# Streamed pieces fetched before the resident sum, square on ScalarE, last tiles transposed one step sooner

## The chip, the cores and the metric

The kernel runs on one NeuronCore of a Trainium2 chip. TensorE multiplies matrices, VectorE, ScalarE and GpSimd work on vectors, and SyncE (SP) issues nearly all transfers between HBM and the core's SBUF. The metric is the device time of one execution in microseconds. Before the change it is 2450.3 us, the median of three runs from 2446.16 to 2452.24.

## The reference

One decoder layer on 2048 tokens of width 1024 (plus 16 meta tokens whose rows are dropped at the end): layer norm, a projection that feeds an S5 state-space mixer and a retention mixer side by side, an output projection, a layer norm, then the MLP that this change is about, and a last layer norm.

```python
h = layer_norm(h, ln_in_g, ln_in_b)
...
    mixed = jnp.concatenate([y_s5, y_ret], axis=-1) @ w_out[l]
    h = layer_norm(DEEPNORM_ALPHA * h + mixed, ln1_g[l], ln1_b[l])
    ff = jnp.square(jax.nn.relu(h @ w_up[l])) @ w_down[l]
    h = layer_norm(DEEPNORM_ALPHA * h + ff, ln2_g[l], ln2_b[l])
return h[:, N_META:]
```

w_up is 1024 x 4096, w_down 4096 x 1024, all in float32.

## The kernel before

**Blocks and phases.** The tokens go through in two blocks of 1024 (eight tiles of 128). Each block runs three phases: the projections and both mixers, the output projection with its layer norm, and the MLP (`phase3`). The order of the work on every engine is written out by the program; there is no scheduler. A counter (`tick`, `defer`) places small jobs between groups of matmuls, and `feed` brings in the weights.

**Products.** Every float32 operand is split into a high part and a rest (`hi`, `lo`), and `mm3` makes three matmuls of each pair. All of them are issued at line 357. A helper casts a weight page to its high part on ScalarE (lines 205, 219) and subtracts on VectorE (lines 207, 220). Line 216 first forms sums of weight pages where a product needs one.

**The MLP.** The 4096 hidden channels are taken in eight groups of four tiles of 128. In each group an up step makes relu(x)^2 of the group's channels for all 1024 tokens, and a down step multiplies these with w_down and adds the result to `acc` for the eight token tiles, two halves each (lines 1453 and 1456). Group 0 is classic (`up_first`): eight outputs of 24 matmuls. Groups 1 to 7 use seven products in place of eight, as Strassen's scheme does (`up_seven`): the products come in the order p = 6, 1, 5, 7, 2, 4, 3, each with two PSUM banks and four pieces k, 24 matmuls in all. Products 6, 7 and 3 read sums of the activations, which `left_sums` forms during group 0's down step and stores to HBM as sums 1 to 4 (line 1312). Sum 1 is needed by every group and is loaded back to stay, over the second half of the first four channel tiles of `h1T` (line 1485, two loads of 1 MB: the resident sum, read by p = 5). Sums 2, 3 and 4 are streamed: `ring_fill` loads pieces of 256 KB, hi and lo, into buffers `q` (line 1345), four pieces for each of p = 6, 7 and 3.

**The square.** `relu2` takes a tile x in SBUF, makes max(x, 0) * x on VectorE (line 1286), casts it on ScalarE (line 1288) and subtracts on VectorE (line 1290). Where the output sits alone in a PSUM bank (all of group 0, and p = 2 of the other groups) ScalarE copies it out first (lines 1277 and 1397). The other outputs are a sum of a bank and a tile, made by VectorE at line 1401.

**The next block.** In the last group of block 0 the down step goes through the token tiles in the order 4, 0, 1, 2, 3, 5, 6, 7 (n = 0 to 7). Beside each step one tile of the next block's h is loaded (line 1437) and after the step it is transposed by TensorE into a PSUM bank `sm` of four (line 339), cast to `hi` by ScalarE (line 340) and subtracted to `lo` by VectorE (line 341). The same steps carry the last layer norm of the finished tiles: VectorE (lines 268, 301), GpSimd (lines 281, 302), ScalarE (line 289) and the store of the output (line 1470). The last tile of the block ends with `norm_end` (lines 310 and 314). Then the next block begins: it loads its `rope` tables, and its first matmuls, the gates of head 0, read the transposed tiles 0 to 3 and then 4 to 7.

**Queues.** SP issues in program order, and each issue waits for what it needs, so a load stands behind every store or load ahead of it. Eight counters (DMAHW0 to 7) are used in turn, so the ninth load after another waits until that one has landed.

Of the kernel before, what the change touches and what calls it, by code (L numbers as in the profile page):

```python
# [12 lines left out]
AF = mybir.ActivationFunctionType  # L13
ALU = mybir.AluOpType
# [15 lines left out]
NT = TB // 128  # L30
# [20 lines left out]
class Builder:  # L51
# [1210 lines left out]
    def up_first(self, b, g):  # L1262

        nc = self.nc
        h1, l1 = self.h1T
        ff = {}
        order = [(f, nb) for f in range(G) for nb in range(2)]
        if g == 0:
            order = [(f, nb) for nb in range(2) for f in range(G)]
        for f, nb in order:  # L1270
            up = self.get(("u", b, g * G + f))
            ps = self.big()
            tk = slice(nb * 512, nb * 512 + 512)
            w = lambda k, i: up[k // 4][:, i, (k % 4) * 128:(k % 4) * 128 + 128]
            self.mm3(ps, [(w(k, 0), w(k, 1), h1[:, k, tk], l1[:, k, tk]) for k in range(8)], marks=(3, 7))
            x = self.q()
            nc.scalar.copy(x, ps)
            ff.setdefault(f, {})[nb] = self.relu2(x)
            if nb == 1:
                self.free(("u", b, g * G + f))  # L1280
        return lambda f, t: [z[:, t % 4 * 128:t % 4 * 128 + 128] for z in ff[f][t // 4]]

    def relu2(self, x):

        nc = self.nc
        nc.vector.scalar_tensor_tensor(out=x, in0=x, scalar=0.0, in1=x, op0=ALU.max, op1=ALU.mult)  # L1286
        hi = self.q(F32R)
        nc.scalar.copy(hi, x)  # L1288
        lo = self.q(F32R)
        nc.vector.tensor_tensor(out=lo, in0=x, in1=hi.bitcast(F32), op=ALU.subtract)  # L1290
        self.qfree()
        return hi, lo
# [55 lines left out]
    def up_seven(self, b, g):  # L1348

        nc = self.nc  # L1350
        V, S = nc.vector, nc.scalar
        h1, l1 = self.h1T
        t1, t2 = slice(0, 512), slice(512, 1024)
        left = {1: (0, t1), 2: (4, t1), 4: (4, t2), 5: (0, t2)}
        NQ = G // 2
        ff = {f: {} for f in range(G)}
        acc, s12, s21, s22 = {}, {}, {}, {}
        for p in PORDER:
            bank = {1: "A", 2: "A", 6: "B", 7: "B", 4: "B", 5: "C", 3: "C"}[p]
            first = p in (1, 6, 5)  # L1360
            for q in range(NQ):
                if first:
                    acc[bank, q] = self.bank()
            w = [self.get(("U", b, g, q, p)) for q in range(NQ)]
            self.hold = p in (4, 3)
            for k in range(4):
                if p in left:
                    k0, tk = left[p]
                    ah, al = h1[:, k0 + k, tk], l1[:, k0 + k, tk]
                else:  # L1370
                    ah, al = self.ring.popleft()
                for q in range(NQ):
                    c = slice(k * 128, k * 128 + 128)
                    self.mm3(acc[bank, q], [(w[q][:, 0, c], w[q][:, 1, c], ah, al)],
                             first=first and k == 0, last=k == 3, more=not first)
                if p not in left:
                    self.qfree(2)
                if self.stream:
                    self.ring_fill((4 if self.bg else 6) if self.stream[0][0] != 2 else 3 if p == 3 else 0)
                if k == 1:  # L1380
                    self.tick()
            for q in range(NQ):
                self.free(("U", b, g, q, p))
                ps, fa, fb = acc[bank, q], 2 * q, 2 * q + 1
                if p == 6:
                    s12[q] = self.q()
                    S.copy(s12[q], ps)
                elif p == 1:
                    s21[q] = self.q()
                    V.tensor_tensor(out=s12[q], in0=s12[q], in1=ps, op=ADD)  # L1390
                    S.copy(s21[q], ps)
                elif p == 5:
                    s22[q] = self.q()
                    V.tensor_tensor(out=s22[q], in0=s21[q], in1=ps, op=ADD)
                elif p == 2:
                    x = self.q()
                    S.copy(x, ps)
                    ff[fa][0] = self.relu2(x)
                else:
                    x, f, h = {7: (s22, fb, 1), 4: (s21, fa, 1), 3: (s12, fb, 0)}[p]  # L1400
                    V.tensor_tensor(out=x[q], in0=x[q], in1=ps, op=ADD)
                    ff[f][h] = self.relu2(x.pop(q))
            self.tick()
        return lambda f, t: [z[:, t % 4 * 128:t % 4 * 128 + 128] for z in ff[f][t // 4]]

    def phase3(self, b):
        nc, a = self.nc, self.a
        ng = NF // G
        nc0 = CLASSIC
        more = b + 1 < NB  # L1410
# [4 lines left out]
        for g in range(ng):  # L1415
# [5 lines left out]
            last = g == ng - 1  # L1421
            ff = self.up_first(b, g) if g < nc0 else self.up_seven(b, g)
# [9 lines left out]
            xs = deque()  # L1432

            def load_h(t):
                xs.append([self.q(), self.q()])
                for hf in range(2):
                    nc.sync.dma_start(out=xs[-1][hf], in_=self.h_d[(b + 1) * NT + t][:, hf * 512:hf * 512 + 512])
            if last and more:
                load_h(to[0])
            for n, t in enumerate(to):  # L1440
                if g >= nc0 and not last and more and n == 4 and rest:
                    self.bg.append(self.rest_norm([rest.popleft() for _ in range(2)]))
                self.hold = g >= nc0 and n == 0
                if last and more and n + 1 < NT:
                    load_h(to[n + 1])
                end = last and n == NT - 1
                for hf in range(2):
                    ps = self.big() if last else self.bank()
# [8 lines left out]
                    if end:  # L1457
# [2 lines left out]
                        self.half_stats(st, self.acc[t], hf)  # L1460
                        if hf == 0:
                            self.norm_halves(self.acc[to[n - 1]], gb2)
                    if n == 3 and hf == 1 and not last:
                        self.qfree(8)
                if last:
                    if more:
                        self.to_channels(xs.popleft(), *self.hT, t * 128)
                        self.qfree(2)
                    out = a["out"][b * TB + t * 128:b * TB + (t + 1) * 128, :]
                    store = lambda t=t, out=out: nc.sync.dma_start(out=out, in_=self.acc[t])  # L1470
                    if not end:
# [7 lines left out]
                elif g >= nc0:  # L1479
                    self.ring_fill(3 if n < 3 else 4 if self.bg or more and rest else 6)  # L1480
                elif g == nc0 - 1 and n >= 4 and sums and (not self.bg or n == NT - 1):
                    sums = False
                    self.drain_bg()
                    for i in range(2):
                        nc.sync.dma_start(out=self.h1T[i].bitcast(F32)[:, 0:4, 512:1024],
                                          in_=self.s_d[b][1][:, :, i, :])
                    self.ring_fill(4)
            self.qfree(16 if last else 8)
            for f in range(G):
                self.free(("d", b, g * G + f))  # L1490
            if last:
# [72 lines left out]
```

## Time and profile before

| | value |
|---|---|
| median of three runs | 2450.3 us |
| the profiled execution | 2449.24 us, of which the span is 2447.5 us |
| mean granted clock of TensorE | 0.987 of full |
| TensorE matmul, weight load | 2344.7 us (96%), 2007.5 us (82%) |
| VectorE, ScalarE, GpSimd | 1615.6 us (66%), 668.4 us (27%), 263.4 us (11%) |

The span goes from the first to the last instruction of the profiled execution, and all times in the rows below count from its start. A timeline row gives the start, the time until the merged instructions end, the engine, the line, what is written and read, the count, and in brackets how long the engine was idle before and what ended that. Matmuls overlap, so the starts of successive groups tell more than their ends. A row of waits gives the total, the count and the longest.

### The profile page before, as it was taken

How to read it: one execution, taken by the hardware profiler on the slowest of the kernel's cores; microseconds unless marked ns; L12 is line 12 of the kernel's file. 1: busy time of each engine (PE TensorE's matmuls, PEld its weight loads, DVE VectorE, ACT ScalarE, POOL GpSimd, SP SyncE). 2: the span in 40 equal slices, each digit the busy share in tenths (PEclk: the TensorE clock that was granted, in tenths of full speed). 3: DMA queues.
4: the chain of work that ended last, by engine and by line, in shares of the span. 5: the costliest groups of instructions: out<-in, count | busy, mean ns of one | idle time of the engine just before them, and what ended most of it. 6: DMA issues, size and time to landing. Idle time of an engine off the chain costs nothing. (4 is left out here: it accounts for less than half of the span.)

```text
span 2447.5 us, 31696 instructions
## 1 busy us (share of the span) xinstructions
PE 2344.7 (96%) x11596; PEld 2007.5 (82%) x11596; DVE 1615.6 (66%) x3491; ACT 668.4 (27%) x1431; POOL 263.4 (11%) x334
## 2 busy tenths in 40 slices
PE   6889999899999999999999999999999999999998
PEld 5778889778878888888888999987887888888886
DVE  6867757666867776766585455565686666566657
ACT  3323323222321232123232222222232122212222
POOL 2322222301000000000030011100100000000004
PEclk8999999999999999999999999999999999999999
DMA  5132253352464546453442322234246343434332
GB/s 202 66 103 83 87 116 114 91 169 73 138 241 146 167 161 202 141 165 112 146 164 92 89 75 79 78 101 153 74 139 239 114 155 112 137 113 155 112 129 86
DMA packets 166972, 313.13 MB, mean 128 GB/s; under 512 B 18544, under 2 KB 59280, under 8 KB 166560
## 3 DMA queue, kind: packets, MB, share of 16 engines
q1 hardware_dynamic: 166816, 311.11, 39.4%
q8 instruction: 91, 1.49, 0.3%
q14 instruction: 65, 0.53, 0.1%
HBM read 256.25 MB, written 55.84 MB: 128 GB/s over the span
## 5 line engine op out<-in xcount | busy, mean ns | idle before, releaser
L357 PE MATMUL big<-pg,act 128*128 128x384 f32 x2304 | 457.0, 348 | 0.8 <-ACT act L340 0.6
L357 PE MATMUL big<-act,pg 128*128 128x512 f32 x1632 | 425.1, 395 | 2.4 <-DVE act L341 2.4
L357 PE MATMUL big<-pg,q 128*128 128x512 f32 x1728 | 412.2, 390 | 0.0
L357 PEld LDWEIGHTS big<-pg,act 128*128 128x128 f32 x2304 | 403.4, 192 | 4.7 <-DVE act L341 1.5
L357 PEld LDWEIGHTS big<-pg,q 128*128 128x128 f32 x1728 | 323.8, 188 | 67.1
L357 PEld LDWEIGHTS big<-act,pg 128*128 128x128 f32 x1632 | 303.9, 189 | 66.9 <-DVE act L341 2.9
L357 PE MATMUL sm<-pg,q 128*128 128x512 f32 x1344 | 322.8, 389 | 0.0
L357 PEld LDWEIGHTS sm<-pg,q 128*128 128x128 f32 x1344 | 252.3, 188 | 52.4
L281 POOL TENSOR_TENSOR ln_rs<-ln_rs,mhalf 128x1 f32<-128x1 f32 (+1 forms) x49 | 51.3, 1047 | 1481.5 <-DVE ln_rs L280 1481.4
L357 PE MATMUL sm<-act,pg 128*128 128x512 f32 x672 | 188.7, 389 | 0.0
L357 PE MATMUL big<-pg,yt 128*128 128x512 f32 x768 | 183.2, 397 | 1.6 <-DVE yt L1140 1.5
L207 DVE TENSOR_TENSOR pg<-wraw,pg 128x512 fp32r<-128x512 f32 x238 | 151.6, 688 | 39.7 <-ACT pg L205 39.7
L357 PEld LDWEIGHTS big<-pg,yt 128*128 128x128 f32 x768 | 145.1, 191 | 33.6 <-DVE yt L1140 3.3
L205 ACT CAST pg<-wraw 128x512 fp32r<-128x512 f32 x272 | 153.2, 619 | 68.1 <-DMA wraw<-in_w_down_dram 27.2
L219 ACT CAST pg<-q 128x512 fp32r<-128x512 f32 x112 | 69.4, 622 | 355.8 <-DVE q L216 355.8
L1288 ACT CAST q<-q 128x512 fp32r<-128x512 f32 x128 | 79.5, 621 | 272.3 <-DVE q L1286 257.4
L357 PE MATMUL sm<-q,pg 128*128 128x512 f32 x504 | 144.6, 395 | 7.5 <-DMA q<-sum 4.0
L1456 DVE TENSOR_TENSOR acc<-acc,big 128x512 f32<-128x512 f32 x128 | 87.0, 684 | 94.7 <-PE big L357 94.6
L1290 DVE TENSOR_TENSOR q<-q 128x512 fp32r<-128x512 f32 x128 | 88.7, 693 | 91.9 <-ACT q L1288 89.0
L357 PEld LDWEIGHTS sm<-act,pg 128*128 128x128 f32 x672 | 126.1, 188 | 26.1
L357 PE MATMUL big<-q,pg 128*128 128x512 f32 x504 | 143.8, 394 | 0.0
L220 DVE TENSOR_TENSOR pg<-q,pg 128x512 fp32r<-128x512 f32 x112 | 76.3, 692 | 82.2 <-ACT pg L219 77.8
(235 smaller groups left out, 2915.2 us busy)
## 6 DMA issues: line engine op xcount, KB each, us to landing
q<-sum SPq DMA_DIRECT2D x336, 256.0 KB, 5.3
wraw<-in_wup_dram SPq DMA_DIRECT2D x64, 512.0 KB, 4.0
wraw<-in_w_down_dram SPq DMA_DIRECT2D x64, 512.0 KB, 4.2
wraw<-in_wslab_dram SPq DMA_DIRECT2D x48, 512.0 KB, 3.6
sum<-q SPq DMA_DIRECT2D x64, 256.0 KB, 2.3
smat<-mat SPq DMA_DIRECT2D x32, 256.0 KB, 3.8
wraw<-in_w_out_dram SPq DMA_DIRECT2D x16, 512.0 KB, 3.7
acc<-h SPq DMA_DIRECT2D x16, 512.0 KB, 3.8
```

The source lines that it names most:

```text
L205: nc.scalar.copy(pg[z][:, 0, :], raw[0][:, z * 512:z * 512 + 512])
L207: e.tensor_tensor(out=pg[z][:, 1, :], in0=raw[0][:, z * 512:z * 512 + 512], in1=pg[z].bitcast(F32)[:, 0, :], op=ALU.subtract)
L219: nc.scalar.copy(pg[:, 0, :], x)
L220: self.post.append(lambda: nc.vector.tensor_tensor(out=pg[:, 1, :], in0=x, in1=pg.bitcast(F32)[:, 0, :], op=ALU.subtract))
L281: nc.gpsimd.tensor_tensor(out=rs[:n, 0:1], in0=rs[:n, 0:1], in1=self.mhalf[:n, 0:1], op=ALU.pow)
L357: nc.tensor.matmul(ps, l, r, start=(i == 0), stop=(i == n - 1), skip_group_check=more)
L1288: nc.scalar.copy(hi, x)
L1290: nc.vector.tensor_tensor(out=lo, in0=x, in1=hi.bitcast(F32), op=ALU.subtract)
L1456: nc.vector.tensor_tensor(out=acc, in0=acc, in1=ps, op=ALU.add)
```

## The change

Four things change. Line numbers of the changed kernel are a few higher (`relu2` at 1288 to 1293, `ring_fill` at 1348, the resident sum at 1493).

1. For outputs that sit alone in a bank, `relu2` takes the bank: ScalarE makes Relu out of it and then Square in place; the VectorE product is left out.
2. The first four pieces of sum 2 are fetched before the resident sum.
3. In the last group of block 0 the tiles of the next block are loaded with counts 1, 1, 1, 1, 1, 2, 0, 0 beside the steps n (and one ahead of them). The tile of n = 5 is transposed between that step's halves, the next after it, the last after n = 6.
4. Buffers of the last group are counted free after n = 4 in place of at the end.

```diff
--- before.py
+++ after.py
@@ -1273,17 +1273,20 @@
             tk = slice(nb * 512, nb * 512 + 512)
             w = lambda k, i: up[k // 4][:, i, (k % 4) * 128:(k % 4) * 128 + 128]
             self.mm3(ps, [(w(k, 0), w(k, 1), h1[:, k, tk], l1[:, k, tk]) for k in range(8)], marks=(3, 7))
-            x = self.q()
-            nc.scalar.copy(x, ps)
-            ff.setdefault(f, {})[nb] = self.relu2(x)
+            ff.setdefault(f, {})[nb] = self.relu2(ps=ps)
             if nb == 1:
                 self.free(("u", b, g * G + f))
         return lambda f, t: [z[:, t % 4 * 128:t % 4 * 128 + 128] for z in ff[f][t // 4]]
 
-    def relu2(self, x):
+    def relu2(self, x=None, ps=None):
 
         nc = self.nc
-        nc.vector.scalar_tensor_tensor(out=x, in0=x, scalar=0.0, in1=x, op0=ALU.max, op1=ALU.mult)
+        if ps is None:
+            nc.vector.scalar_tensor_tensor(out=x, in0=x, scalar=0.0, in1=x, op0=ALU.max, op1=ALU.mult)
+        else:
+            x = self.q()
+            nc.scalar.activation(out=x, in_=ps, func=AF.Relu)
+            nc.scalar.activation(out=x, in_=x, func=AF.Square)
         hi = self.q(F32R)
         nc.scalar.copy(hi, x)
         lo = self.q(F32R)
@@ -1393,9 +1396,7 @@
                     s22[q] = self.q()
                     V.tensor_tensor(out=s22[q], in0=s21[q], in1=ps, op=ADD)
                 elif p == 2:
-                    x = self.q()
-                    S.copy(x, ps)
-                    ff[fa][0] = self.relu2(x)
+                    ff[fa][0] = self.relu2(ps=ps)
                 else:
                     x, f, h = {7: (s22, fb, 1), 4: (s21, fa, 1), 3: (s12, fb, 0)}[p]
                     V.tensor_tensor(out=x[q], in0=x[q], in1=ps, op=ADD)
@@ -1435,14 +1436,19 @@
                 xs.append([self.q(), self.q()])
                 for hf in range(2):
                     nc.sync.dma_start(out=xs[-1][hf], in_=self.h_d[(b + 1) * NT + t][:, hf * 512:hf * 512 + 512])
+            def turn():
+                self.to_channels(xs.popleft(), *self.hT, nt.popleft() * 128)
+                self.qfree(2)
+            nt, nl = deque(to), deque(to)
             if last and more:
-                load_h(to[0])
+                load_h(nl.popleft())
             for n, t in enumerate(to):
                 if g >= nc0 and not last and more and n == 4 and rest:
                     self.bg.append(self.rest_norm([rest.popleft() for _ in range(2)]))
                 self.hold = g >= nc0 and n == 0
-                if last and more and n + 1 < NT:
-                    load_h(to[n + 1])
+                if last and more:
+                    for _ in range((1, 1, 1, 1, 1, 2, 0, 0)[n]):
+                        load_h(nl.popleft())
                 end = last and n == NT - 1
                 for hf in range(2):
                     ps = self.big() if last else self.bank()
@@ -1460,12 +1466,13 @@
                         self.half_stats(st, self.acc[t], hf)
                         if hf == 0:
                             self.norm_halves(self.acc[to[n - 1]], gb2)
-                    if n == 3 and hf == 1 and not last:
+                    if n == 3 + last and hf == 1:
                         self.qfree(8)
+                    if last and more and n == 5 and hf == 0:
+                        turn()
                 if last:
-                    if more:
-                        self.to_channels(xs.popleft(), *self.hT, t * 128)
-                        self.qfree(2)
+                    if more and n < NT - 1:
+                        turn()
                     out = a["out"][b * TB + t * 128:b * TB + (t + 1) * 128, :]
                     store = lambda t=t, out=out: nc.sync.dma_start(out=out, in_=self.acc[t])
                     if not end:
@@ -1481,11 +1488,11 @@
                 elif g == nc0 - 1 and n >= 4 and sums and (not self.bg or n == NT - 1):
                     sums = False
                     self.drain_bg()
+                    self.ring_fill(4)
                     for i in range(2):
                         nc.sync.dma_start(out=self.h1T[i].bitcast(F32)[:, 0:4, 512:1024],
                                           in_=self.s_d[b][1][:, :, i, :])
-                    self.ring_fill(4)
-            self.qfree(16 if last else 8)
+            self.qfree(8)
             for f in range(G):
                 self.free(("d", b, g * G + f))
             if last:
```

On SP, at the end of group 0's down step of block 0, before the change (the last stores of the sums; `act` is `h1T`, and a counter named in brackets is waited for):

```order
L1312 DMA sum0_2_127<-q_7050 128x512 [waits DMAHW0_49,Activation_49]
L1312 DMA sum0_2_127<-q_7052 128x512 [waits DMAHW1_49,DVE_49]
L1312 DMA sum0_4_129<-q_7056 128x512 [waits DMAHW2_49,Activation_49]
L1312 DMA sum0_4_129<-q_7058 128x512 [waits DMAHW3_49,DVE_49]
L1485 DMA act_5798<-sum0_1_126 128x4x512 [waits DMAHW4_49,PE_49]
L1485 DMA act_5799<-sum0_1_126 128x4x512 [waits DMAHW5_49]
L1345 DMA q_7093<-sum0_2_127 128x512 [waits DMAHW6_49]
L1345 DMA q_7094<-sum0_2_127 128x512 [waits DMAHW7_49]
```

The same place with the change:

```order
L1315 DMA sum0_4_129<-q_7058 128x512 [waits DMAHW3_49,DVE_49]
L1348 DMA q_7091<-sum0_2_127 128x512 [waits DMAHW4_49,PE_49]
L1348 DMA q_7092<-sum0_2_127 128x512 [waits DMAHW5_49]
L1348 DMA q_7095<-sum0_2_127 128x512 [waits DMAHW6_49]
L1348 DMA q_7096<-sum0_2_127 128x512 [waits DMAHW7_49,PE_49]
L1348 DMA q_7099<-sum0_2_127 128x512 [waits DMAHW0_49]
L1348 DMA q_7100<-sum0_2_127 128x512 [waits DMAHW1_49,PE_49]
L1348 DMA q_7103<-sum0_2_127 128x512 [waits DMAHW2_49]
L1348 DMA q_7104<-sum0_2_127 128x512 [waits DMAHW3_49]
L1493 DMA act_5798<-sum0_1_126 128x4x512 [waits DMAHW4_49]
L1493 DMA act_5799<-sum0_1_126 128x4x512 [waits DMAHW5_49]
```

The two loads of the resident sum moved behind the eight loads of sum 2, and they now wait for the counters of the first two of these (DMAHW4 and 5). Block 1 has the same order.

On TensorE, in the last group of block 0 (`sm<-ident,q` are transposes of the next block's tiles, `big<-pg,q` the down step, `big<-act,pg` the next block's gates), the difference:

```order
 L357 MATMUL big<-pg,q 128x512 x24
 L339 MATMUL sm<-ident,q 128x128 x8
-L357 MATMUL big<-pg,q 128x512 x24
+L357 MATMUL big<-pg,q 128x512 x12
+L339 MATMUL sm<-ident,q 128x128 x8
+L357 MATMUL big<-pg,q 128x512 x12
 L339 MATMUL sm<-ident,q 128x128 x8
 L357 MATMUL big<-pg,q 128x512 x24
 L339 MATMUL sm<-ident,q 128x128 x8
 L357 MATMUL big<-pg,q 128x512 x24
-L339 MATMUL sm<-ident,q 128x128 x8
 L357 MATMUL big<-act,pg 128x512 x48
```

The last eight transposes no longer stand right before the gates; eight stand inside step n = 5 instead.

On VectorE, the end of block 0 before the change (the adds of steps n = 6 and 7, and the split halves of the transposed tiles at line 341):

```order
L1456 TENSOR_TENSOR acc<-acc,big 128x512 x2
L341 TENSOR_TENSOR act<-sm,act 128x4x128 x2
L268 BN_STATS ln_st<-acc 128x6 x2
L279 BN_AGGR ln_mv<-ln_st 128x2
L280 TENSOR_SCALAR ln_rs<-ln_mv 128x1
L301 TENSOR_TENSOR acc<-acc,q 128x512 x2
L1456 TENSOR_TENSOR acc<-acc,big 128x512
L268 BN_STATS ln_st<-acc 128x6
L301 TENSOR_TENSOR acc<-acc,q 128x512 x2
L1456 TENSOR_TENSOR acc<-acc,big 128x512
L268 BN_STATS ln_st<-acc 128x6
L341 TENSOR_TENSOR act<-sm,act 128x4x128 x2
```

And with the change:

```order
L1462 TENSOR_TENSOR acc<-acc,big 128x512 x2
L341 TENSOR_TENSOR act<-sm,act 128x4x128 x2
L268 BN_STATS ln_st<-acc 128x6 x2
L279 BN_AGGR ln_mv<-ln_st 128x2
L280 TENSOR_SCALAR ln_rs<-ln_mv 128x1
L301 TENSOR_TENSOR acc<-acc,q 128x512 x2
L1462 TENSOR_TENSOR acc<-acc,big 128x512
L268 BN_STATS ln_st<-acc 128x6
L301 TENSOR_TENSOR acc<-acc,q 128x512 x2
L1462 TENSOR_TENSOR acc<-acc,big 128x512
L268 BN_STATS ln_st<-acc 128x6
```

The split of the last tile, at the end before, is now the pair behind the adds of step n = 6; the pair that stood there moved one step up.

## Rows read from the trace of the kernel before

**Rows 1.** The page: busy time, share of the span and instructions of each engine

```profile
PE 2344.7 (96%) x11596; PEld 2007.5 (82%) x11596; DVE 1615.6 (66%) x3491; ACT 668.4 (27%) x1431; POOL 263.4 (11%) x334
```

**Rows 2.** Waits of TensorE over the span: total us, times, longest us

```profile
PE sm L357 <- DMA q<-sum: 4.0, 2, 3.8
PE sm L357 <- DVE q L216: 3.5, 1, 3.5
PE big L357 <- DVE act L341: 2.4, 1, 2.4
```

**Rows 3.** Timeline, TensorE, end of group 0 in block 0

```profile
687.63 2.88 PE L357 MATMUL sm<-pg,q 128*128 128x512 f32 x12
690.35 2.88 PE L357 MATMUL big<-pg,q 128*128 128x512 f32 x12
696.99 1.25 PE L357 MATMUL sm<-q,pg 128*128 128x512 f32 x3 [3.75 <-DMA q<-sum]
...
704.47 0.84 PE L357 MATMUL sm<-act,pg 128*128 128x512 f32 x3
```

**Rows 4.** Windows: us, engines' busy us, PEclk, DMA share, GB/s

```profile
698.00:700.00 2.00, 2.00 (x8) 1.54 (x7) 0.00 (x0) 0.00 (x0) 0.00 (x0) 0.57 1.05 396
```

**Rows 5.** Timeline, SP and TensorE, end of group 0 in block 1

```profile
1853.01 1.25 SPq L1485 DMA_DIRECT2D act<-sum  x2
...
1856.34 2.88 PE L357 MATMUL big<-pg,q 128*128 128x512 f32 x12
...
1862.69 0.76 PE L357 MATMUL sm<-q,pg 128*128 128x512 f32 x1 [3.46 <-DVE q L216]
...
1871.56 0.84 PE L357 MATMUL sm<-act,pg 128*128 128x512 f32 x3
```

**Rows 6.** Lines 1345 and 1485 around 690 us, issue ns, landing; 1345 overall

```profile
L1345 SPq DMA_DIRECT2D q<-sum x6: 425/624/737, 688.5 to 691.7; - x6
...
DMA to landing us min/median/max: 8.1/8.3/8.5
...
L1485 SPq DMA_DIRECT2D act<-sum x2: 539/589/639, 687.2 to 687.8; - x2
...
DMA to landing us min/median/max: 6.1/7.2/8.3
...
q<-sum SPq DMA_DIRECT2D x336, 256.0 KB, 5.3
```

**Rows 7.** Timeline and loads, end of block 0 and start of block 1

```profile
1260.74 5.74 PE L357 MATMUL big<-pg,q 128*128 128x512 f32 x24
1265.99 1.29 DVE L341 TENSOR_TENSOR act<-sm,act 128x512 fp32r<-128x512 f32 x2 [0.75 <-ACT act L340]
1267.11 5.74 PE L357 MATMUL big<-pg,q 128*128 128x512 f32 x24
1276.22 1.28 DVE L1456 TENSOR_TENSOR acc<-acc,big 128x512 f32<-128x512 f32 x2
1279.84 5.96 PE L357 MATMUL big<-act,pg 128*128 128x512 f32 x25
1287.50 1.27 DVE L341 TENSOR_TENSOR act<-sm,act 128x512 fp32r<-128x512 f32 x2
1295.19 6.43 PE L357 MATMUL big<-pg,act 128*128 128x384 f32 x36
...
L1437 SPq DMA_DIRECT2D q<-h x2: 383/640/896, 1261.1 to 1261.5; - x2
...
DMA to landing us min/median/max: 4.6/4.7/4.8
...
L552 SPq DMA_DIRECT2D rope<-in_rope_dram x1: 399/399/399, 1292.2 to 1292.2; - x1
```

**Rows 8.** Groups by line: names, shapes, count, busy us, mean ns, idle before

```profile
L1286 DVE SCALAR_TENSOR_TENSOR q<-q 128x512 f32<-128x512 f32 x128 | 88.2, 689 | 2.9
L1288 ACT CAST q<-q 128x512 fp32r<-128x512 f32 x128 | 79.5, 621 | 272.3 <-DVE q L1286 257.4 <-DMA q<-sum 12.8 <-DMA q<-h 2.1
```

## The prediction

> **What bounds the kernel now.** The page's first line says it: TensorE has a matmul under way for 96% of the span, VectorE 66%, ScalarE 27% [rows 1]. So nothing that is saved on VectorE or ScalarE counts by itself; only TensorE's gaps do, and what follows each gap. The second view is the list of what TensorE waited for. In the stages that the diff touches it holds three gaps of over 2 us [rows 2]: one for a piece of a sum from HBM (3.8 us), one put down to VectorE line 216 (3.5 us), one for the split halves of the next block's transposed tiles (2.4 us).
>
> The third view, the timeline, places the gaps. The first [rows 3]: down groups start every 2.72 us (687.63, 690.35), so the next work, p = 6, was due at 693.07. It began at 696.99, waiting for q<-sum. Then the granted clock fell: 0.57 in the stretch shown [rows 4], which is TensorE at the 1.2 GHz level for most of it. The 24 matmuls of p = 6 need 2 x 2.72 = 5.44 us at the 2.4 GHz level; the first matmul of p = 1 came at 704.47. Loss: 704.47 - 693.07 - 5.44 = 5.96 us.
>
> The second gap is the same place in block 1 [rows 5]: due at 1856.34 + 2.72 = 1859.06, p = 1 at 1871.56, so 1871.56 - 1859.06 - 5.44 = 7.06 us. The table blames VectorE here (3.46 us), but line 216 makes a weight page for later p, and SP's start at 1853.01 lies as far ahead of the gap as in block 0. I read it as the same DMA wait.
>
> Why the piece is late [rows 3, 6]: SP issued the two loads of the resident sum (1 MB each) at 687.2 and 687.8, the first piece at 688.5. They landed 6.1 and 8.3 us after issue; the six loads behind them took 8.1 to 8.5, so the first was there near 696.8. Over the run such a load takes 5.3 us in the median.
>
> The third gap [rows 7]: the next block's gates start at 1279.84 and need 4 x 2.72 = 10.88 us, so the following matmuls were due at 1290.72. They came at 1295.19: 4.47 us lost. TensorE waited 2.4 us for line 341, which VectorE ran at 1287.50, since it is half a step and more behind: it added step n = 6 at 1276.22, whose matmuls began at 1267.11 and took 5.74 us, to 1272.85.
>
> The gaps that can go hold 5.96 + 7.06 + 4.47 = 17.49 us.
>
> **The change part by part.**
>
> *Pieces before the resident sum.* Nothing is added; eight loads pass two. I take SP's start from the profile, 687.2. The issues there took up to 0.74 us each [rows 6], so the second load of the first pair starts by 688.0 and the eighth by 692.4. A load of this size behind one store landed 4.6 us after issue [rows 7], the median is 5.3: the first pair is there at 692.6 to 693.3, the last by 697.7. They are due at 693.07 and 693.07 + 3 x 1.36 = 697.15. Between no wait and one of 0.2 + 0.5 us I take none, since the issues are slowest when the queue holds the 2 MB. In block 1 SP starts at 1853.01 for work due at 1859.06, so there is as much room.
>
> What is late next is the resident sum, which p = 5 reads after p = 6 and p = 1, at 693.07 + 10.88 = 703.95. In the order of the change its loads wait for the counters of the first pair and stand behind eight issues, so they go out at 693.3 and 693.9 at the latest. With the longest landing measured, 8.3, they are in by 702.2: 1.7 us to spare, in block 1 about the same. The pieces of sums 3 and 4 go out after them as before. So both losses go: 13.0 us; at the dear end 0.7 us is given back twice.
>
> *Square on ScalarE.* 16 outputs in the classic group and 28 in the p = 2 steps, 44 of 128. Each drops a VectorE operation of 689 ns (44 x 0.689 = 30.3 us) and adds a ScalarE pass; the cast of the same tile there takes 621 ns, so 44 x 0.62 = 27 us on an engine that is idle 73% of the span [rows 1, 8]. The copy out of the bank becomes a Relu out of the bank. The trace of before has no Square; the bounds are that it is free, or that it takes a cast's time twice, 54 us of ScalarE. On TensorE I cost either at nothing: the list of its waits has none for these tiles, and the p = 2 outputs are needed two more p (10.9 us) and a down step later. If the longer ScalarE row made a weight cast late the cost would be one pass, 0.6 us. The gain is bounded by 8 x 0.69 = 5.5 us of earlier sums per block, since VectorE is behind while it makes them; it widens the margins above, so I add nothing.
>
> *Tiles transposed sooner.* The number of transposes stays; two are done inside and after n = 5, one after n = 6, none after n = 7. For the last tile, line 341 now stands behind the adds of step 6: these began at 1276.22, and 1.4 us for the two halves moved ahead of them, 1.3 for the adds and 1.3 of its own make 1280.2. The second gate needs it at 1279.84 + 5.44 = 1285.28. Even three such pairs later it is in time. The loss of 4.47 us goes.
>
> What is late next there: (a) the tile for the second transposing of n = 5. SP issues it at 1261.1 and 1261.5, behind the store, and it took 4.6 to 4.8 us there: 1265.9 to 1266.3; needed at 1260.74 + 5.44 + 0.92 = 1267.1 (0.92 is what a step's transposes cost: 6.37 between step starts less 5.44). Margin 0.8. (b) The bank for it, free when line 341 has run on the tile of n = 4: 1265.99 to 1267.28. That is level with the need: 0 to 0.5 us. (c) rope, which SP loads behind the last store, at 1292.2: with the same 4.7 it lands near 1296.9. The first tile of head 0 now ends 4.47 us sooner, at 1290.72 + 6.43 x 24/36 = 1295.0, and TensorE wants it rotated after half a tile more, 1297.1, with the rotation between: 0 to 1 us. I take 0.5 us for (b) and (c) together, of 0 to 1.5.
>
> *Sum.* 17.5 - 0.5 = 17.0 us of the profiled execution's 2449.24 (span 2447.5 and some 1.7 around it): 2432.2. That execution is 1.1 us under the median of 2450.3, so the median goes to 2433.3. The uncertain part is the clock: of the losses 3.75, 3.46 and 2.4 us are idle time, so 2.2, 3.6 and 2.1 us are the slower matmuls behind them. A repeat may draw three times the least or the most of these, 6.3 to 10.8 in place of 7.9, which moves the gain to 15.4 to 19.9.
>
> The Trainium skill (TensorE: Matmul & The Clock Gate, Part 1) says that the monitor behind this clock is not aligned with the program, so that the number of slow matmuls after a gap differs from run to run. The trace bears this out as far as it goes: the 3.46 us gap cost more clock than the 3.75 us one. By that rule a median of other executions could hold less of the 7.9 us than this profile does; with none of it, the sum would be 17.0 - 7.9 = 9.1 us.
>
> **Rivals.**
> 1. *Only the two sum gaps go* (or the transposes give back their part): the mid-step transposes meet a tile or bank that is later than (a) and (b), and a gap as long as the third one comes there, with its clock. For it: margins of 0 to 0.8 us, and VectorE a step behind. Against it: line 341 for the last tile comes some 8 us earlier than before (1280.2 for 1288.8). Gain 17.0 - 4.5 = 12.5: 2437.8.
> 2. *Pieces and resident sum share the rate after all.* 4 MB must arrive within 17 us, and each p needs 512 KB per 1.36 us. If each block keeps a gap of 2.4 us with 2.2 to 3.6 of clock, 2 x 5.3 = 10.6 comes back: 6.4 us gain, 2443.9. For it: the loads took 8.3 us when the queue was full. Against: the first pieces now meet no 2 MB.
> 3. *The change doesn't do what it says:* the late piece waits for its stores, not for the 2 MB ahead of it. Then both gaps stay and 4.0 us remain: 2446.3. Against it: the landing times above, equal for act and piece.
> 4. *Slower:* the resident sum, now behind the pieces, comes after p = 5 wants it, and p = 5 is stopped in both blocks. The price is (w + 2.7) twice, w the lateness; it decides at 2 x (w + 2.7) > 17.0 + 7.4, so w above 9.5 us: landing 20 us after issue in place of 6.1 to 8.3. With w = 10: 2 x 12.7 - 17.0 = 8.4 us slower, 2458.7. For it: only that nothing in the profile shows these loads behind eight others.
>
> **How the numbers follow.** Forecast 0.70, rival 1 0.15, rival 2 0.06, rival 3 0.06, rival 4 0.03. A difference within 0.3% (7.4 us) can't be told from none here. Faster by more: forecast and rival 1, with a little of rival 2: 0.87. Same: 0.10. Slower: 0.03. The forecast's own range is 2430.4 to 2434.9 by the clock's share, 2427 to 2438 with about 3 us either way for the spread of the runs (2446.16 to 2452.24). Up to rival 2 it is 2427 to 2443.5.
>
> **What would show it.** In the profile after: no gap of TensorE before p = 6 in either block, clock 1.00 in those stretches; act<-sum issued after the eight pieces and landed before p = 5; no wait for line 341 at the gates; 44 Relu and 44 Square passes near 0.6 us on ScalarE and VectorE some 30 us less busy. It is wrong if a wait for act<-sum, for q<-h or for a bank stands in TensorE's list with more than 2 us, or if the clock falls elsewhere.

## The result, and the profile after

The changed kernel takes 2437.34 us (median of 4 runs, 2434.59 to 2439.23), the kernel before, run beside it, 2451.1 us (2446.16 to 2452.24). The ratio is 0.9947 with a 95% interval of 0.993 to 0.9964: 13.8 us less, and between 8.8 and 17.2. The forecast was a gain of 17.0, at the upper edge of that interval.

The profiled execution of the changed kernel took 2439.23 us, span 2437.4. Its busy times, beside [rows 1]:

```profile
PE 2344.9 (96%) x11596; PEld 2012.3 (83%) x11596; DVE 1590.8 (65%) x3447; ACT 697.1 (29%) x1475; POOL 263.1 (11%) x334
```

TensorE's work is the same; 24.8 us went from VectorE, 28.7 came to ScalarE. The line of the square alone lost 30.1 us (88.2 in [rows 8], 58.1 here), as forecast; why VectorE's total fell by less is not traced. The two passes, by line (names, count, busy us, mean ns of one), and the square that stayed on VectorE:

```profile
L1285 DVE SCALAR_TENSOR_TENSOR q<-q 128x512 f32<-128x512 f32 x84 | 58.1, 692 | 2.9
L1289 ACT ACTIVATE q<-q 128x512 f32<-128x512 f32 x44 | 27.8, 633 | 1.4
L1288 ACT ACTIVATE q<-big 128x512 f32<-128x512 f32 x30 | 17.8, 593 | 16.4 <-PE big L357 13.4 <-DVE acc L328 3.0
L1288 ACT ACTIVATE q<-sm 128x512 f32<-128x512 f32 x14 | 8.2, 589 | 0.0
```

Gap 1, beside [rows 3]. Timeline of TensorE, end of group 0 in block 0 (start us, duration us):

```profile
696.61 2.88 PE L357 MATMUL big<-pg,q 128*128 128x512 f32 x12
699.33 0.84 PE L357 MATMUL sm<-q,pg 128*128 128x512 f32 x3
...
704.77 0.84 PE L357 MATMUL sm<-act,pg 128*128 128x512 f32 x3
```

p = 6 begins 2.72 us after the last down group, and p = 1 follows 5.44 us later: no wait and no slow matmul. The granted clock of the window of p = 6 is 1.00 where [rows 4] had 0.57, at the same transfer rate (us; each engine's busy us; PEclk, DMA share, GB/s):

```profile
700.00:702.00 2.00, 2.00 (x10) 1.67 (x9) 1.86 (x4) 0.62 (x1) 0.00 (x0) 1.00 1.05 396
```

SP's queue there, and how long the pieces took from issue to landing (issue ns, first and last issue):

```profile
689.49 4.14 SPq L1348 DMA_DIRECT2D q<-sum  x8
693.68 1.65 SPq L1493 DMA_DIRECT2D act<-sum  x2
...
L1348 SPq DMA_DIRECT2D q<-sum x8: 376/430/719, 689.5 to 692.9; - x8
...
DMA to landing us min/median/max: 4.1/5.3/6.0
```

The first piece leaves 699.33 - 689.49 = 9.84 us ahead of its use (before: SP began with the resident sum 5.83 us ahead) and lands in 6.0 at most, in place of over 8 [rows 6]. In block 1 the lead is 9.84 us again, and p = 6 runs through, beside [rows 5]:

```profile
1846.25 4.71 SPq L1348 DMA_DIRECT2D q<-sum  x8
...
1856.09 0.84 PE L357 MATMUL sm<-q,pg 128*128 128x512 f32 x3
...
1861.53 0.84 PE L357 MATMUL sm<-act,pg 128*128 128x512 f32 x3
```

Gap 3, beside [rows 7]: the gates of block 1 run through, 1280.01 to 1290.88, and the wait for line 341 is gone. But a new wait stands 8 us behind. TensorE, then VectorE and SP:

```profile
1280.01 11.04 PE L357 MATMUL big<-act,pg 128*128 128x512 f32 x48
1290.88 6.43 PE L357 MATMUL big<-pg,act 128*128 128x384 f32 x36
1299.00 0.30 PE L663 MATMUL sm<-ident,qk 128*128 128x128 f32 x1 [1.69 <-DVE qk L654]
...
1297.57 0.42 DVE L651 TENSOR_TENSOR t<-big,rope 128x256 f32<-128x256 f32 x1 [1.41 <-DMA rope<-in_rope_dram]
...
1292.06 0.99 SPq L316 DMA_DIRECT2D out_dram<-acc  x2
1293.15 0.41 SPq L552 DMA_DIRECT2D rope<-in_rope_dram  x1
```

The rope table still leaves SP behind the last stores, and now VectorE waits for it. Ahead of the gates TensorE also waits 1.73 us for the fifth tile (q<-h). That wait is not new: it took 1.21 us in the kernel before and 1.67 in its second profile.

**How the executions were compared.** The spans of the two profiles differ by only 10.1 us, since this one came to the first up projection of block 0 at 610.48 us, the kernel before at 604.22, and the change leaves all the code up to there alone. So only stretches between two marks are compared, and what a kernel without that wait needs is taken as zero. These are: from the first up projection of block 0 (the mark) to p = 1, 94.29 us; the gates, 10.87; from there to the second rotated transposes, 11.13; from the first transposes of acc in block 1 to p = 1 there, 151.39. What each execution needed beyond that, in us, idle time and slow matmuls together:

```
kernel                       mark   gap 1  gates  rope  gap 2  mark to end
before                       604.22  5.96   4.48  0.00   7.04   1843.3
before again                 607.30  3.75   4.19  0.00   5.98   1840.5
order alone                  608.82  0.00   2.62  0.02   0.00   1829.7
square alone                 606.36  0.48   4.25  0.03   1.11   1831.6
tiles alone                  606.07  6.45   0.01  2.10   5.71   1837.9
tiles alone, again           608.37  5.24   0.01  2.30   5.99   1839.2
changed                      610.48  0.00   0.00  1.86   0.00   1826.9
changed again                605.69  0.00   0.01  3.96   0.00   1828.6
changed without order        605.63  0.50   0.01  0.03   1.14   1828.8
changed without tiles        608.48  0.00   2.30  0.00   0.00   1829.5
changed, rope on ScalarE     606.33  0.00   0.01  1.18   0.00   1826.5
the same again               608.13  0.01   0.01  1.12   0.00   1823.7
rope, and feed held          605.05  0.01   0.01  0.03   0.00   1830.6
rope, and tile load ahead    607.95  0.00   0.01  1.26   0.00   1826.0
```

### The profile page after: what moved, and what is told of

Its sections match the earlier page's. It is cut to its first block, busy times and chain, and to the rows that moved or that the text cites. A ratio compares the mean times of both kernels' runs of the same rounds, so it can differ in the third digit from the quotient of the medians.

```text
span 2437.4 us, 31642 instructions
## 1 busy us (share of the span) xinstructions
PE 2344.9 (96%) x11596; PEld 2012.3 (83%) x11596; DVE 1590.8 (65%) x3447; ACT 697.1 (29%) x1475; POOL 263.1 (11%) x334
## 5 line engine op out<-in xcount | busy, mean ns | idle before, releaser
L357 PE MATMUL big<-pg,act 128*128 128x384 f32 x2304 | 463.6, 351 | 0.8 <-ACT act L340 0.6
L357 PEld LDWEIGHTS big<-pg,act 128*128 128x128 f32 x2304 | 410.2, 195 | 4.6 <-issue 1.4
```

Source lines behind the costliest of these rows:

```text
L357: nc.tensor.matmul(ps, l, r, start=(i == 0), stop=(i == n - 1), skip_group_check=more)
```

## The experiments

Theory A is the prediction's sum: the order of the loads closes gaps 1 and 2, the tiles gap 3, the square adds nothing. Theory B came from the trace after: the square brings the sums some 4 us forward, and that by itself would close most of gaps 1 and 2. Part 4 of the change (buffers counted free sooner) goes with the tiles in every run below; the prediction gave it no price, and no run shows it alone.

**1. Order alone.** In the kernel before:

```diff
                     self.drain_bg()
+                    self.ring_fill(4)
                     for i in range(2):
                         nc.sync.dma_start(out=self.h1T[i]..., in_=self.s_d[b][1][:, :, i, :])
-                    self.ring_fill(4)
```

> Only the order: the pieces of the streamed sum are fetched ahead of the resident sum, square and tile schedule as before. Theory A (the order is what closes the two waits before p = 6): both waits go, 5.96 us in block 0 and 7.06 us in block 1, so about 13.0 us less than before (2438); the SyncE queue issues the first piece 5.8 to 6.1 us ahead of p = 6, as before's first load was. Theory B (the earlier sums do most of it): a piece issued 5.8 us ahead that lands 5.3 to 8.5 us after its issue is still up to 2.5 us late, so PE waits up to 2.5 us in each block and the gain is 8 to 13 us (2438 to 2443). The wait of the gates on the ScalarE chain (4.47 us in before) stays under both.

2439.15 us against 2448.15, ratio 0.9957 (0.9944 to 0.9969): 9.0 us less. Both gaps are gone. SP, the landing of the pieces, and TensorE:

```profile
691.13 3.83 SPq L1345 DMA_DIRECT2D q<-sum  x8
...
DMA to landing us min/median/max: 3.7/5.4/6.0
...
697.67 0.84 PE L357 MATMUL sm<-q,pg 128*128 128x512 f32 x3
```

6.54 us of lead and 6.0 of landing at most. In block 1 the lead was 5.94, the landing 5.5. So A is right on the order and B's doubt falls: it suffices without the square, but only just. By size, 9.0 us is short of A's 13.0; the interval reaches from 7.6 to 13.7.

In block 1 p = 6 now begins before VectorE has run line 216 at all, which [rows 2] blamed for that gap:

```profile
1857.03 0.84 PE L357 MATMUL sm<-q,pg 128*128 128x512 f32 x3
...
1857.84 0.69 DVE L216 TENSOR_TENSOR q<-wraw 128x512 f32<-128x512 f32 x1
```

**2. Square alone.** In the kernel before, the outputs out of a bank:

```diff
-            x = self.q()
-            nc.scalar.copy(x, ps)
-            ff.setdefault(f, {})[nb] = self.relu2(x)
+            ff.setdefault(f, {})[nb] = self.relu2(ps=ps)
...
+            nc.scalar.activation(out=x, in_=ps, func=AF.Relu)
+            nc.scalar.activation(out=x, in_=x, func=AF.Square)
...
```

(and the same for p = 2).

> Only Relu and Square on ScalarE in place of the square on VectorE; order of the loads and tile schedule as before. Theory A: nothing (2449 to 2451), both waits before p = 6 stay 2 us or longer because the resident sum still stands ahead of the pieces. Theory B: the last sums are stored about 4 us sooner, so the first load leaves SyncE 9.8 us ahead of p = 6 instead of 5.8 to 6.1; the first piece, 1.3 to 1.7 us behind it, lands 8.1 to 8.5 us later, hence 0 to 0.5 us late: most of both waits goes by this part alone, 12 to 13 us less than before (2437 to 2439).

2439.78 us against 2448.15, ratio 0.996 (0.9947 to 0.9974): 8.4 us less. Theory A's "adds nothing" is wrong for the part by itself, and B's 12 to 13 is more than the median shows. In block 1, with the resident sum still ahead:

```profile
1845.69 1.29 SPq L1486 DMA_DIRECT2D act<-sum  x2
1847.04 14.86 SPq L1348 DMA_DIRECT2D q<-sum  x17
...
DMA to landing us min/median/max: 8.4/8.9/9.0
...
1856.12 1.32 PE L357 MATMUL sm<-q,pg 128*128 128x512 f32 x3 [0.43 <-DMA q<-sum]
```

The pieces are as slow as before, 9.0 us at most, but leave 8.65 us ahead of their use at 1855.69: 0.43 us late.

**3. The changed kernel without the order:**

```diff
                     self.drain_bg()
-                    self.ring_fill(4)
...
+                    self.ring_fill(4)
```

> The changed kernel with the order undone: resident sum ahead of the pieces again, square on ScalarE and tile schedule kept. Theory A: both waits before p = 6 come back, about 13 us over the changed kernel (2450). Theory B: the first piece leaves 8.2 us ahead of p = 6 and lands 0 to 0.5 us late, so 0 to 1.5 us over the changed kernel (2437 to 2439).

2437.02 us against 2448.15, ratio 0.9951 (0.9938 to 0.9963), the changed kernel's ratio within the error: A's 2450 is wrong, B's 2437 to 2439 holds. Gaps 1 and 2 hold 0.50 and 1.14 us. So in this kernel either of the two parts nearly replaces the other: their gains overlap, they don't add. Its rope cost nothing, because the gates began 2 us late: the table left SP 0.26 us after the gates' end (1288.72 and 1288.46), in the changed kernel 2.27 us after it (1293.15 and 1290.88). The gates were late because the matmuls behind the wait for the fifth tile were slow, 12 in 4.54 us in place of 3.01:

```profile
1255.73 1.44 PE L339 MATMUL sm<-ident,q 128*128 128x128 f32 x8 [2.05 <-DMA q<-h]
1256.83 4.54 PE L357 MATMUL big<-pg,q 128*128 128x512 f32 x12
```

**4. Tiles alone**, in the kernel before (loads and transposes of the next block's tiles as in the change):

```diff
-                if last and more and n + 1 < NT:
-                    load_h(to[n + 1])
+                if last and more:
+                    for _ in range((1, 1, 1, 1, 1, 2, 0, 0)[n]):
+                        load_h(nl.popleft())
...
+                    if last and more and n == 5 and hf == 0:
+                        turn()
...
```

> Only the next block's tiles are loaded and transposed a step sooner; order and square as before. The 4.47 us wait of the gates at the end of block 0 goes under every theory. Theory A (prediction): the rope tables cost up to 1.5 us of it, taken at 0.5, so about 4.0 us less than before (2446 to 2447). Theory B (after's trace): the rope tables still leave behind the last stores, and PE waits 1.7 us for them, so 3.0 to 3.2 us less (2447 to 2448). The two waits before p = 6 stay at their length in before. If the transposes gave their part back elsewhere, 0 (2450 to 2451).

2448.96 us against 2448.15, ratio 1.0003 (0.9994 to 1.0012). That was a miss for both theories, so it was run again.

> Only the tile schedule, once more (its first timing gave 0, where its trace had lost the wait of the gates and the kernel without this part lay 3.4 us over the changed one). Theory B (the part is worth 3 us by itself, and the first timing was a low draw of before or a high one of it): 2 to 4 us less than before run beside it. Theory C (it gives its gain back when VectorE still squares): 0 again, and then this profile shows the return between the gates of block 1 and the end.

2447.51 us against 2449.02, ratio 0.9993 (0.9984 to 1.0002). In both traces the wait of the gates is gone and TensorE waits for the rotation instead; the second one's:

```profile
1283.73 11.04 PE L357 MATMUL big<-act,pg 128*128 128x512 f32 x48
...
1303.17 0.30 PE L663 MATMUL sm<-ident,qk 128*128 128x128 f32 x1 [2.13 <-DVE qk L654]
```

By the table the part gains 2.3 to 4.5 us at the gates and gives 1.9 to 4.0 back at the rope (nothing in one execution), where 0 to 1.5 was foreseen. What is left, about 1.5 us (means in the next section), is too little for these runs to tell from none. That something else takes the rest is neither shown nor excluded.

**5. The changed kernel without the tiles,**

```diff
-                if last and more:
-                    for _ in range((1, 1, 1, 1, 1, 2, 0, 0)[n]):
-                        load_h(nl.popleft())
+                if last and more and n + 1 < NT:
+                    load_h(to[n + 1])
...
```

beside **the changed kernel again**, unedited:

> The changed kernel without the earlier loads and transposes of the next block's tiles (order and square kept). Theory A (prediction's terms): the gates wait 4.5 us again and the rope's 0.5 is saved, 4.0 us over the changed kernel. Theory B (after's trace: the rope wait takes 1.3 of it): 2.7 to 3.2 us over. Theory C (as the run with that part alone was timed): 0. By the trace all three show the wait of the gates on L341, 2.2 to 2.4 us in the profile.

> The changed kernel once more, for its spread and a second profile. No edit. If the 6.3 us by which the changed kernel's first up projection of block 0 began later than in before (610.5 against 604.2 us, in code that the change leaves alone) is a matter of the execution, this profile shows it anywhere between 604 and 611 us, and the rest of the span (from there to the end) is 1827 us again, within 1.5. If it belongs to the changed kernel, it is 610 again.

2438.08 us without the tiles (ratio 0.9958, 0.9944 to 0.9972), 2434.68 with them (0.9945, 0.9932 to 0.9957): 3.4 us apart, with overlapping intervals. So these runs do not decide between the 4.0, the 2.7 to 3.2 and the 0 of the three theories. The changed kernel's second run repeats its gain, 14.5 us of 2449.16. Its mark lay at 605.69 this time, so 610.48 belonged to the execution. The stretch from the mark to the end was 1828.6, 1.7 longer than in the first profile: here the wait for the rotation was followed by slow matmuls, 12 in 3.85 us, and the rope cost 3.96 in all.

```profile
1294.53 0.30 PE L663 MATMUL sm<-ident,qk 128*128 128x128 f32 x1 [2.21 <-DVE qk L654]
1294.69 3.85 PE L357 MATMUL big<-pg,act 128*128 128x384 f32 x12
```

Without the tiles the gates waited for line 341 again, but more cheaply than before:

```profile
1278.02 5.96 PE L357 MATMUL big<-act,pg 128*128 128x512 f32 x25
1285.83 5.53 PE L357 MATMUL big<-act,pg 128*128 128x512 f32 x23 [1.86 <-DVE act L341]
1291.19 6.43 PE L357 MATMUL big<-pg,act 128*128 128x384 f32 x36
```

**6. The kernel before again**, unedited:

> The kernel before, once more, for a second profile; no edit. The first up projection of block 0 begins anywhere between 604 and 611 us if that spread belongs to the execution, and at 604 if it belongs to the kernel; from there to the end 1843 us within 2. Both waits before p = 6 and the 4.5 us at the gates are there again.

2448.56 us against 2449.02, ratio 0.9998 (0.9989 to 1.0006). The mark is at 607.30, and from there to the end it took 1840.5 us, a little under the range foreseen. The same three gaps are there, at other prices: gap 1 took 3.75 us in place of 5.96. Its timeline:

```profile
693.44 2.88 PE L357 MATMUL big<-pg,q 128*128 128x512 f32 x12
699.38 1.29 PE L357 MATMUL sm<-q,pg 128*128 128x512 f32 x3 [3.06 <-DMA q<-sum]
700.51 0.85 PE L357 MATMUL big<-q,pg 128*128 128x512 f32 x3
```

After 3.06 us of idling three matmuls were slow; in [rows 3] it took twelve and more to come back (p = 6 lasted 7.48 us in place of 5.44).

**7. The rope table on the ScalarE queue**, in the changed kernel, for block 1:

```diff
-        nc.sync.dma_start(out=self.rope, in_=a["rope"][b])
+        e = nc.scalar if b else nc.sync
+        e.dma_start(out=self.rope, in_=a["rope"][b])
         self.mask = p1.tile([128, 128], F32, name="mask")
-        nc.sync.dma_start(out=self.mask, in_=a["mask"])
+        e.dma_start(out=self.mask, in_=a["mask"])
```

> The changed kernel with block 1's rope table and mask loaded from the ScalarE queue (issued after the last tile's scaling, at about 1285.5 us) and no longer from SyncE behind the last stores (1293.2 us). If the new wait of the first rotated transposes (1.7 us on DVE) is the table's landing, it goes to 0.3 us or less, and the kernel is 1.3 us faster than the changed one. Rival: the ScalarE queue stands at the issue until the table's memory is free, and the gate activations behind it come late: 0 to 4 us slower.

2433.55 us, ratio 0.9938 (0.9925 to 0.995); the changed kernel beside it had 2434.68. ScalarE did stand at the issue until VectorE had left the table's memory, 6.5 us, but TensorE waited for nothing that stood behind it. VectorE, after the edit (lines are one higher):

```profile
1290.89 1.22 DVE L201 TENSOR_TENSOR wu<-wraw,wu 128x1024 fp32r<-128x1024 f32 x1
1292.03 0.42 DVE L652 TENSOR_TENSOR t<-big,rope 128x256 f32<-128x256 f32 x1
...
1293.32 0.29 DVE L654 TENSOR_TENSOR qk<-t,t 128x128 f32<-128x128 f32 x1 [0.54 <-DMA out_dram<-acc]
```

VectorE's wait for the table is gone, as foreseen. TensorE's wait at the rotation only went from 1.69 to 0.98 us, not to 0.3, and 1.1 to 1.2 us of its loss stays (in 7 again too): VectorE is busy with its queue until the rotation begins, and then waits for a store of acc. So in these runs the table was the last thing the rotation waited for, but not the only late one.

**8. The feed held for a step as well** (one more line on top of 7):

```diff
-                self.hold = g >= nc0 and n == 0
+                self.hold = g >= nc0 and n == 0 or last and more and n == 2
```

> As the run before, and the two weight loads that stand ahead of the fifth tile's load on SyncE go behind it (no feed in the step n = 2 of the last group). The fifth tile leaves 2 us or more sooner, and the 1.7 us wait of its transposes goes: 3.0 us less than the changed kernel in all. Rival: the weight page made one step later is late for the next block's gates, a new wait on PE at 1280 us, and the gain is 1.3 or less.

2437.52 us, ratio 0.9957 (0.9944 to 0.9969): 4.0 slower than 7, worse than either theory. SP and TensorE:

```profile
1251.71 2.14 SPq L178 DMA_DIRECT2D wraw<-in_wu_dram  x2
1253.94 0.86 SPq L1439 DMA_DIRECT2D q<-h  x2
...
1260.02 1.94 PE L339 MATMUL sm<-ident,q 128*128 128x128 f32 x8 [3.86 <-DMA q<-h]
1261.61 4.90 PE L357 MATMUL big<-pg,q 128*128 128x512 f32 x12
```

The fifth tile no longer waits; the sixth does, since the two weight loads now stand ahead of it, and they stand on SP for their buffer until 1251.7. The wait is 3.86 us in place of the fifth tile's 1.67 in 7, and the 12 matmuls behind it took 4.90 us in place of 3.00.

**9. Only the tile load moved ahead of the weight loads** on SP (on top of 7), beside **7 again**:

```diff
...
+                    self.raw_ok = n != 2
+                    if n == 3:
+                        self.feed_raw()
```

> The changed kernel with the rope table on the ScalarE queue, and on SyncE the fifth tile's load moved ahead of the two weight loads that stood before it; the casts on ScalarE and VectorE keep their places. The 1.5 to 2.1 us wait of that tile's transposes goes, and no later tile waits: 1.7 us less than the same kernel without the move (run beside it), 3 us less than the changed kernel (2431 to 2432). Rival: the next tile waits in its place, as in the run where the feed was held, 0 to 3 us slower.

> The changed kernel with the rope table on the ScalarE queue, once more, beside the run above: 0.993 to 0.994 of before again, the wait of the first rotated transposes under 0.5 us.

2434.04 us (0.9937, 0.9925 to 0.9949) with the move, 2432.41 (0.9933, 0.9921 to 0.9945) without: no gain. The tile's wait went to 0.15 us. The next tile's transposes then found VectorE late with the bank that they write, which is what the prediction's (b) had in mind, 0.61 us:

```profile
1259.27 1.21 PE L339 MATMUL sm<-ident,q 128*128 128x128 f32 x8 [0.15 <-DMA q<-h]
...
1263.85 1.25 PE L339 MATMUL sm<-ident,q 128*128 128x128 f32 x8 [0.61 <-DVE act L341]
```

From p = 1 to the gates it took 574.53 us, 7 again 574.55. The wait of TensorE at the rotation in 7 again was 0.95 us, and not under 0.5. The runs with the table on ScalarE and the feed as it was (7, 7 again and 9) have the lowest ratios here, 0.9933 to 0.9938. Where 7 and the changed kernel stood side by side the difference was 1.1 us, which is within their spread.

## Why the prediction was right, and by how much it was off

**Gaps 1 and 2: right in mechanism.** The piece was late because of the 2 MB ahead of it. Taking the 2 MB away shortened the landing from over 8 us to 3.7 to 6.0 (experiment 1), and both gaps closed. VectorE line 216, which the table of waits blamed in block 1, had no part in it: with the order alone that wait is gone, and p = 6 begins before the line has run. In one profile with the gap left in (tiles alone, again) the table itself names the piece:

```profile
1864.04 0.47 PE L357 MATMUL sm<-q,pg 128*128 128x512 f32 x1 [3.60 <-DMA q<-sum]
```

The pieces took 6.0 us at most, where the prediction worked with 4.6 to 5.3. SP's lead of 5.94 to 6.54 us in the order alone leaves next to no room over that, though no wait came; in the changed kernel the square's earlier sums made the lead 9.84.

**The resident sum** was not late. Its four loads landed in 7.7 to 9.7 us, at about 704 in block 0, and p = 5 begins at 699.33 + 10.88 = 710.21. In block 0:

```profile
L1493 SPq DMA_DIRECT2D act<-sum x2: 518/544/569, 693.7 to 694.8; - x2
...
DMA to landing us min/median/max: 8.1/8.9/9.7
```

Rivals 2, 3 and 4 fall with that and with experiment 1, where SP's stores were done at about the same time as before (its lead was 6.54 and 5.94 us in the two blocks, before 5.83 and 6.05): no gap before p = 6 from a shared rate or from the stores, nothing at p = 5.

**"It widens the margins above, so I add nothing"** held for the whole change, whose gaps the order would have closed anyway, but it hid that the same gain could be had twice: the square alone gave 8.4 us, the order alone 9.0, both and the tiles 13.8 to 14.5.

**Gap 3 and (c).** The wait for line 341 went, and (a) and (b) cost nothing: no wait stands at the mid-step transposes. Experiment 9 shows that (b) was close: with the fifth tile's wait down to 0.15 us, 0.61 us of it came. The term that failed is "0.5 us for (b) and (c) together": the rope cost 1.86 and 3.96 us in the changed kernel's two profiles, beyond the bound of 1.5. SP's issue came at 1293.15 instead of 1292.2, as VectorE's last chain ended later, and the table landed at 1297.45 instead of 1296.9. As experiment 7 shows, VectorE's own queue and a store of acc would have cost over 1 us even with the table there in time. That is rival 1 by a smaller amount and at another place. And the term had no clock in it: of the 3.96 us, 2.21 were idle and most of the rest slow matmuls, so the sign "the clock falls elsewhere" did come in that execution. The number alone does not decide against that rival: 13.8 and 14.5 lie nearer its 12.5 than the forecast's 17.0. The traces do decide: the third gap went, and no other came at the transposes.

**The clock share** was the other mis-sized term. The sum took 5.96, 7.06 and 4.47 us from one profile. Where the gap was left in, the profiles here gave: gap 1 5.96, 3.75, 6.45, 5.24, mean 5.35; gap 2 7.04, 5.98, 5.71, 5.99, mean 6.18; gates 4.48, 4.19, 2.62, 4.25, 2.30, mean 3.57. With the rope of the five kernels that have the tiles and load it on SP (2.10, 2.30, 1.86, 3.96, 0.03, mean 2.05) the sum is 5.35 + 6.18 + 3.57 - 2.05 = 13.05 us, against 13.8 and 14.5 measured. From the mark to the end the two profiles of the changed kernel are 14.2 us shorter than the two of before, about 1 us more than that sum. By the sum the forecast's 17.0 was 3.9 too much: 2.4 from the prices of one execution, 1.5 from the rope. Of the 15.1 us that the three gaps cost on average 9.5 were idle time and 5.6 slow matmuls, where the prediction had 7.9 for the latter; in no profile did all three gaps come without them. The prediction gave 15.4 to 19.9 for the clock's draw; its low end was too high, since a gap can cost little more than its idle time (3.75 us with 3.06 idle in before again).

## What to carry to other kernels

A loss behind a late transfer can have several cures whose gains don't add: before pricing a part, ask what it would do alone and what is left when the other has done it. Take the price of a gap, wait and slow matmuls together, from several executions, since one profile draws it. And where a wait on the bounding engine is removed, look at what the next instruction's operands wait for on SP: here over half of the third gap's gain, 2.05 of 3.57 us on average, went back at the next place that waited. A table of waits names one releaser for each wait; where two conditions end close together, an edit that moves only one of them tells which it was.

## What the runs showed of the hardware

The same idle time does not cost the same clock. Waits of 2.43 and 2.34 us at the gates were followed by a granted clock of 0.50, the 1.2 GHz level; waits of 2.19 and 1.86 us there by 1.00, the 2.4 GHz level. The first full windows of 2 us behind the wait, in before (it ended at 1288.23) and with the order alone (at 1286.74):

```profile
1290.00:1292.00 2.00, 2.00 (x6) 0.50 0.42 166
```

```profile
1288.00:1290.00 2.00, 2.00 (x10) 1.00 0.63 252
```

Six matmuls against ten in the same time. Length alone does not order them: the 2.05 us wait for the fifth tile in experiment 3 was followed by slow matmuls, 12 in 4.54 us; a wait of the same length for the same tile in experiment 1 was not:

```profile
1258.49 1.27 PE L339 MATMUL sm<-ident,q 128*128 128x128 f32 x8 [2.06 <-DMA q<-h]
1259.52 5.72 PE L357 MATMUL big<-pg,q 128*128 128x512 f32 x24
```

No run here shows what decides it. The Trainium skill (TensorE: Matmul & The Clock Gate, Part 1) says that the monitor's windows run freely and do not start with the program; the trace agrees in that the price of gap 1 moved between 3.75 and 6.45 us over four executions, with waits of 3.06 to 3.75 us. What the Trainium skill says there of the number of slow matmuls, it says of the start of a kernel; that the number differs behind a gap too, as the prediction took it to, is what these rows show.

Landing times follow what stands ahead in the queue: a 256 KB piece took 3.2 to 6.0 us with nothing large ahead of it (the eight loads in each block of the changed kernel and of the order alone), and the first four to six behind the two 1 MB loads took 8.1 to 9.0 ([rows 6] and experiment 2). The two large loads took 6.1 to 9.1 us ahead of the pieces (before, square alone) and 7.7 to 10.7 behind them (changed, order alone); nothing waited for that, since p = 5 comes 10.88 us after p = 6.
